# Third layer's modulation moved from the second feed-forward into the second layer's value projection

## The chip, the cores and the metric

The kernel runs on one core of a Trainium2 chip. The metric is the device time of one launch in microseconds. The kernel before took 1823.88 us in the median of three runs (1822.57 to 1826.66).

## What is computed

Three layers act on a sequence of 512 tokens of width 1024, with batch 1. Layers 0 and 1 have a mixer and a feed-forward part; layer 2 is a hybrid of attention and a state-space model. Each layer is modulated: a vector computed from a condition `c` scales, shifts and gates the activations.

```python
# layers 0 and 1
mod = silu(c) @ ada_w[i] + ada_b[i]                 # 1024 -> 6 * 1024
sh1, sc1, g1, sh2, sc2, g2 = split(mod, 6)
x = x + g1 * mixer(rms_norm(x) * (1 + sc1) + sh1)   # i = 0: banded attention; i = 1: spatial gating
x = x + g2 * (square(relu(h @ w1)) @ w2)            # h = rms_norm(x) * (1 + sc2) + sh2
# mixer of layer 1
z = gelu(h @ w_in); u, v = split(z, 2)              # 1024 -> 3072 and 3072
y = (u * (W_s rms_norm(v) + b_s)) @ w_out
# layer 2
mod = silu(c_2) @ w_ada + b_ada                     # 1024 -> 3 * 1024
shift, scale, gate = split(mod, 3)
x = x + gate * (concat(attention(h), state_space(h)) @ w_out)
```

The modulation of layer 2 depends on `c_2` alone and is needed only when the norm of layer 2 begins. The tables of the state-space model (powers of exp(lambda dt), and their products with b and c) depend on weights alone and are needed in layer 2.

## The kernel before

All of x lies transposed in on-chip memory as eight tiles `xT` of 128 features by 512 tokens. Large products are made in three passes: each operand is split into a high and a low part, and `mm3` issues high*high, low*high and high*low (lines 145, 146 and 147). Weights come in chunks of 128 x 1024 by `wchunk`: a DMA on SP's queue into one of four `raw` buffers (L156), a copy by ACT that rounds to the high part `wh` (L157), and a subtraction by DVE that leaves the low part `wl` (L160). `wh` and `wl` have three buffers each, so a chunk is prepared when the one three before it has been used.

A unit of modulation (`ada_cols`) makes 512 of its columns on DVE. A DMA brings weights into `araw`; for each of the eight blocks of 128 rows DVE multiplies by the condition and adds to an accumulator in an `nrm_t` buffer (L196 for the first block, L198 for seven more), and one reduction (L200) leaves partial sums. After every second unit `ada_fold` adds them across partitions by two small matmuls (L208) and adds the bias (L211). How many row blocks one DMA brings (`kchunk`) and how many buffers there are (`abufs`) is set by the stage: 4 and 2 in the feed-forward of layer 0, 1 and 2 in that of layer 1. Layer 2 has six units, so 48 DMAs of 256 KB, 6 of L196, 42 of L198, 6 of L200 and 3 folds.

Such units are background work. `n.work` is a list of functions, and a stage calls `bg()` at certain places, which takes the next function from the list and emits its instructions there. The feed-forward of layer 1 calls it after each group of 256 hidden columns (four times in each of four groups) and after each pair of output blocks. In the kernel before its list holds the units of layer 2's modulation, the folds, and 13 units for the state-space tables: `s5_base`, and for each of four sets `s5_set` parts 0, 1 and 2. `s5_base` is a long chain of small operations on DVE that ends in copies, with some products on POOL. Part 0 is products on POOL (L970, L971, and L972 over a whole tile). Part 1 starts with transposes on TensorE (L977) that read POOL's tile `s5_B`, and later has matmuls L990. Part 2 is a recurrence on POOL and a DMA of the tables to DRAM (L1012). The set's tiles have one buffer each.

The place where a function is called gives its instructions their rank. The framework then fixes one order for each engine from an estimated timeline (`schedule_with_timeline_sim`, L1571); on the chip each engine works through its own order and waits at an instruction whose operands are not there. An instruction of low rank may thus be ordered ahead of later-called work when its buffers and inputs are free early.

In layer 1 `layer1` first makes the values: six blocks `cb` of 512 columns, each of four weight chunks `kk`, four token blocks and two rows (L717); the gelu (L720) and a sum of squares on DVE (L722) follow each block. Then come the units u with the spatial product (L746), whose results go into `g_H` and `g_L`, eight buffers each, and the output product. The value stage has no background work in the kernel before. `then_hybrid` (L641) is what reads layer 2's modulation first.

Of the kernel before, what the change touches and what calls it, by code (L numbers as in the profile page):

```python
# [11 lines left out]
F32 = mybir.dt.float32  # L12
# [7 lines left out]
T = 512  # L20
# [87 lines left out]
class Net:  # L108
    def __init__(self, tc, ctx, d):
        self.tc, self.nc, self.d = tc, tc.nc, d  # L110
        self.ctx = ctx
        self.pp = ctx.enter_context(tc.tile_pool(name="pp", bufs=1))
        self.wp = ctx.enter_context(tc.tile_pool(name="wp", bufs=1))
        self.sp = ctx.enter_context(tc.tile_pool(name="sp", bufs=2))
        self.dr = ctx.enter_context(tc.tile_pool(name="dr", bufs=1, space=bass.MemoryType.DRAM))
        self.s5d = [self.dr.tile([128, self.S5W], F32, name=f"s5d{a}") for a in range(4)]
        self.ps = ctx.enter_context(tc.tile_pool(name="ps", bufs=1, space=bass.MemoryType.PSUM))
        self.work = []
        self.apool = None
        self.mod = {}  # L120


# [58 lines left out]
    def ada_cols(self, w, cond, b, bias, out):  # L181

        nc = self.nc
        wr = w.rearrange("(k p) n -> p k n", p=128)
        acc = self.sp.tile([128, T], F32, name="nrm_t")
        kc = self.kchunk
        cv = self.sp.tile([128, 32], F32, name="a_v")[:, 0:8]
        nc.vector.tensor_copy(cv, cond)
        cond = cv
        for h in range(0, KT, kc):  # L190
            v = self.apool.tile([128, kc, T], F32, name="araw", tag="araw", bufs=self.abufs)
            nc.sync.dma_start(v, wr[:, h:h + kc, b * 128:b * 128 + T])
            for i in range(kc):
                k = h + i
                if k == 0:
                    nc.vector.tensor_scalar(acc, v[:, i, :], cond[:, 0:1], None, op0=ALU.mult)  # L196
                else:
                    nc.vector.scalar_tensor_tensor(acc, v[:, i, :], cond[:, k:k + 1], acc, op0=ALU.mult, op1=ALU.add)  # L198

        nc.vector.tensor_reduce(self.folds[:, b // 8 % 2, b % 8:b % 8 + 4, :], acc.rearrange("p (i q c) -> p i q c", i=4, q=4),  # L200
                                axis=AX.X, op=ALU.add, apply_transpose=True)
        if b % 8 == 4:
            self.folding = lambda: self.ada_fold(b - 4, bias, out)
# [442 lines left out]
    def ffn(self, l, then, hold=None):  # L646
        nc, d, tc = self.nc, self.d, self.tc
        mod = self.mods[l]
        w1 = d["ffn_w1"][l].rearrange("(k p) n -> p k n", p=128)
        w2 = d["ffn_w2"][l].rearrange("(k p) n -> p k n", p=128)  # L650
        with ExitStack() as c:
            self.abufs, self.kchunk = (2, 4) if l == 0 else (2, 1)
            fp = self.apool = c.enter_context(tc.tile_pool(name="fp", bufs=1))
            banks = itertools.cycle(["a", "a", "s", "s", "t", "t"])
            for g in range(4):
                gh, gl = [], []
                for m4 in range(4):
                    c0 = g * 1024 + m4 * 256
                    if c0 == 0:
                        accs = self.up_first([(w1[:, :, 0:512], 0)], banks)  # L660
                    elif c0 == 256:
                        accs = []
                    else:
                        ws = [self.wchunk(w1[:, 4 * hf:4 * hf + 4, c0:c0 + 256], 4, 256) for hf in range(2)]
                        accs = self.up(ws, banks)
                    for acc in accs:
                        s = fp.tile([128, T], F32, name="f_s", bufs=3)
                        H = fp.tile([128, T], F32R, name="f_H", bufs=9)
                        L = fp.tile([128, T], F32R, name="f_L", bufs=9)
                        nc.scalar.activation(s, acc, AF.Relu)  # L670
                        nc.vector.scalar_tensor_tensor(s, acc, 0.0, s, op0=ALU.max, op1=ALU.mult)
                        nc.scalar.copy(H, s)
                        nc.vector.tensor_tensor(L, s, H.bitcast(F32), op=ALU.subtract)
                        gh.append(H)
                        gl.append(L)
                    self.bg()
                self.fold()
                for m2 in range(4 if g < 3 else 2):
                    ws = [self.wchunk(w2[:, g * 8 + 4 * hf:g * 8 + 4 * hf + 4, m2 * 256:m2 * 256 + 256], 4, 256)
                          for hf in range(2)]  # L680
                    self.down(m2, lambda k, mi: [x[:, k % 4, mi * 128:mi * 128 + 128] for x in ws[k // 4]],
                              lambda k: (gh[k], gl[k]), 8, mod[:, 40:48], banks)
                    self.bg()
            self.bg(100)
            hold = hold or (lambda m: [fp.tile([128, 1024], F32R, name="w_last", bufs=6) for _ in range(2)])
            self.down_last(w2[:, 24:32, :], lambda k: (gh[k], gl[k]), 8, mod[:, 40:48], banks, then(), hold)


    def layer1(self):
        nc, d, tc = self.nc, self.d, self.tc  # L690
# [1 line left out]
        w_in = d["b_w_in"][0].rearrange("(k p) n -> p k n", p=128)  # L692
        w_out = d["b_w_out"][0].rearrange("(k p) n -> p k n", p=128)
        with ExitStack() as c:
            gp = c.enter_context(tc.tile_pool(name="gp", bufs=1))
            v = [gp.tile([128, 3072], F32, name=f"v{i}") for i in range(4)]
            wsT = gp.tile([128, 8, 128], F32, name="wsT")
            bsb = gp.tile([128, 8, 128], F32, name="bsb")
# [6 lines left out]
            for cb in range(6):  # L705
# [5 lines left out]
                for kk in range(4) if cb else ():  # L711
                    w = self.wchunk(w_in[:, 2 * kk:2 * kk + 2, c0:c0 + 512], 2, 512)
                    for i in range(4):
                        for k2 in range(2):
                            k = 2 * kk + k2
                            self.mm3(accs[i], self.h(k, i * 128, i * 128 + 128), [x[:, k2, :] for x in w],
                                     k == 0, k == KT - 1)  # L717
                for i in range(4):
                    vv = v[i][:, cb * 512:cb * 512 + 512]
                    nc.scalar.activation(vv, accs[i], AF.Gelu)  # L720
# [811 lines left out]
def body(tc, out, **d):  # L1532
    with ExitStack() as ctx:
        n = Net(tc, ctx, d)
# [3 lines left out]
        ada += [lambda b=b: n.ada_layer(1, b) for b in range(12)]  # L1538
        n.work = [f for a in ada for f in (a, n.fold)]
        n.ffn(0, n.then_layer1)  # L1540
        n.layer1()
        with tc.tile_pool(name="s5p", bufs=1) as sp5:
            ada = [f for b in range(6) for f in (lambda b=b: n.ada_layer(2, b), n.fold)]
            s5 = [lambda: n.s5_base(sp5)] + [lambda a=a, q=q: n.s5_set(sp5, a, q) for a in range(4) for q in range(3)]

            n.work = s5[:1] + ada[:3] + s5[1:2] + ada[3:5]
            n.work += [f for p in zip(s5[2:9], ada[5:]) for f in p] + s5[9:]
            held = []

            def hold(m):  # L1550
# [24 lines left out]
```

## Time and profile before

| | |
|---|---|
| median of three runs | 1823.88 us |
| the profiled execution | 1823.5 us, span 1821.3 us |
| TensorE (PE) busy | 1769.0 us, 97% |
| DVE busy | 1126.9 us, 62% |
| ACT, POOL busy | 652.4 us, 453.8 us |
| mean granted TensorE clock | 0.993 of full |

The stages on the span's clock, in us: layer 0 to about 310, its feed-forward to 680, layer 1's values 680 to 820, units and output 820 to 1105, its feed-forward 1105 to 1490, layer 2 from there. A matmul's busy time overlaps the next one's, so the distance from start to start tells the rate: where nothing is missing a 128x512 matmul starts every 0.234 us.

In a windows row the columns are: the stretch, its length, then busy us and instruction count (x) of PE, of PE's weight loads (PEld), DVE, ACT and POOL, then the granted clock, the DMA engines' share and GB/s. In a timeline row: start, duration, engine, line, operation, output and inputs, count, and in brackets the idle time before it and who ended it.

### The profile page before, as it was taken

The numbers are of one execution on the slowest core, as the hardware profiler recorded it, in microseconds if no ns is written. First come the engines' busy times: TensorE is split into PE (matmuls) and PEld (weight loads), VectorE is DVE, ScalarE is ACT, GpSimd is POOL, SyncE is SP. The second block draws the span as 40 slices with busy tenths as digits, with TensorE's granted clock in tenths as the row PEclk, the third lists the DMA queues.
The fourth block names the chain that finished last, engine by engine and source line by source line (L and its number), as shares of the span: only waits on it lengthen the run. The fifth ranks groups of instructions, "written<-read, shape, count | busy, mean of one in ns | idle before, by whom it ended". The sixth has DMA issues, their size and how long they took to land.

```text
span 1821.3 us, 24858 instructions
## 1 busy us (share of the span) xinstructions
PE 1769.0 (97%) x9308; PEld 1418.1 (78%) x9308; DVE 1126.9 (62%) x2153; ACT 652.4 (36%) x1159; POOL 453.8 (25%) x625
## 2 busy tenths in 40 slices
PE   7999999999999999999999999998999999999998
PEld 4787767887788888888888889886888888786556
DVE  4477866887763445345344457996565554698864
ACT  3345545413231334222223244223233434245642
POOL 0055632000000020001011020048877420144340
PEclk9999999999999999999999999999999999999999
DMA  9554514677643333322322333653444344553101
GB/s 340 168 171 121 172 53 128 196 253 255 221 139 93 104 104 93 93 90 64 102 93 73 105 113 119 196 174 127 140 139 139 125 148 140 172 167 106 47 12 47
DMA packets 197975, 243.06 MB, mean 133 GB/s; under 512 B 18912, under 2 KB 151264, under 8 KB 196192
## 3 DMA queue, kind: packets, MB, share of 16 engines
q1 hardware_dynamic: 194464, 229.77, 40.2%
q10 hardware_dynamic: 3392, 11.71, 1.8%
q8 instruction: 73, 1.20, 0.3%
q14 instruction: 46, 0.38, 0.1%
HBM read 228.87 MB, written 12.58 MB: 133 GB/s over the span
## 4 chain that ended last, share of the span: by engine, by line
PE 77%; DVE 9%; DMA 6%; issue 3%; POOL 2%; ACT 2%; SPq 0%; ACTq 0%; DVEq 0%; POOLq 0%
PE ps_a L145 10%; PE ps_a L146 9%; PE ps_a L147 9%; PE ps_s L146 7%; PE ps_s L145 6%; PE ps_s L147 6%; PE ps_t L146 6%; PE ps_t L145 6%; PE ps_t L147 6%; DMA araw<-in_ada_w 3%; DVE nrm_t L198 2%; DVE wl L160 2%; DMA araw<-in_w_ada 1%; PE ps_s L1474 1%; PE ps_s L592 1%
## 5 line engine op out<-in xcount | busy, mean ns | idle before, releaser
L160 DVE TENSOR_TENSOR wl<-raw,wh 128x1024 fp32r<-128x1024 f32 (+3 forms) x269 | 326.7, 1215 | 277.4 <-ACT wh L157 273.3
L157 ACT ACTIVATE wh<-raw 128x1024 fp32r<-128x1024 f32 (+3 forms) x269 | 275.8, 1025 | 516.3 <-PE ps_a L146 135.7
L146 PE MATMUL ps_a<-hL,wh 128*128 128x512 f32 (+1 forms) x440 | 165.3, 378 | 2.7 <-DVE hL L312 2.3
L145 PE MATMUL ps_a<-hH,wh 128*128 128x512 f32 (+1 forms) x440 | 165.6, 387 | 2.4 <-ACT hH L311 0.8
L147 PE MATMUL ps_a<-hH,wl 128*128 128x512 f32 (+1 forms) x440 | 163.4, 376 | 0.0
L198 DVE SCALAR_TENSOR_TENSOR nrm_t<-araw,a_v,nrm_t 128x512 f32<-128x512 f32 x182 | 143.5, 791 | 28.2 <-DMA araw<-in_ada_w 17.5
L145 PE MATMUL ps_a<-wh,hH 128*128 128x256 f32 (+2 forms) x392 | 125.5, 322 | 2.4 <-ACT hH L311 2.1
L254 POOL TENSOR_TENSOR sq<-sq 128x512 f32<-128x512 f32 x15 | 22.5, 1497 | 411.3 <-ACT sq L250 411.3
L753 POOL TENSOR_TENSOR g_t<-g_t,g_u 128x512 f32<-128x512 f32 x24 | 35.2, 1486 | 358.1 <-DVE g_t L749 352.6
L146 PE MATMUL ps_a<-wl,hH 128*128 128x256 f32 (+2 forms) x392 | 122.6, 313 | 0.7 <-DVE wl L160 0.7
L147 PE MATMUL ps_a<-wh,hL 128*128 128x256 f32 (+2 forms) x392 | 120.0, 311 | 0.0
L146 PE MATMUL ps_s<-hL,wh 128*128 128x512 f32 (+1 forms) x288 | 101.3, 358 | 0.0
L147 PE MATMUL ps_s<-hH,wl 128*128 128x512 f32 (+1 forms) x288 | 101.3, 358 | 0.0
L145 PE MATMUL ps_s<-hH,wh 128*128 128x512 f32 (+1 forms) x288 | 97.3, 359 | 0.0
L145 PEld LDWEIGHTS ps_a<-hH,wh 128*128 128x128 f32 x440 | 81.0, 188 | 20.7 <-issue 2.5
L145 PE MATMUL ps_t<-hH,wh 128*128 128x512 f32 (+1 forms) x248 | 96.8, 390 | 0.0
L146 PEld LDWEIGHTS ps_a<-hL,wh 128*128 128x128 f32 x440 | 83.1, 189 | 17.5 <-DVE hL L312 2.7
L146 PE MATMUL ps_t<-hL,wh 128*128 128x512 f32 (+1 forms) x248 | 96.7, 390 | 0.0
L147 PE MATMUL ps_t<-hH,wl 128*128 128x512 f32 (+1 forms) x248 | 96.0, 389 | 0.0
L147 PEld LDWEIGHTS ps_a<-hH,wl 128*128 128x128 f32 x440 | 82.9, 188 | 15.9
L145 PEld LDWEIGHTS ps_a<-wh,hH 128*128 128x128 f32 x392 | 74.0, 189 | 18.4 <-issue 9.8
L320 DVE SCALAR_TENSOR_TENSOR xT<-ps_a,mod,xT 128x512 f32<-128x512 f32 (+1 forms) x65 | 44.7, 691 | 60.2 <-PE ps_a L147 60.1
(576 smaller groups left out, 4296.9 us busy)
## 6 DMA issues: line engine op xcount, KB each, us to landing
raw<-in_ffn_w SPq DMA_DIRECT2D x128, 512.0 KB, 3.8
araw<-in_ada_w SPq DMA_DIRECT2D x28, 1024.0 KB, 5.8
raw<-in_b_w_in SPq DMA_DIRECT2D x48, 512.0 KB, 3.7
araw<-in_ada_w SPq DMA_DIRECT2D x64, 256.0 KB, 3.3
raw<-in_a_w_in SPq DMA_DIRECT2D x28, 512.0 KB, 4.0
raw<-in_b_w_out SPq DMA_DIRECT2D x32, 384.0 KB, 3.0
araw<-in_w_ada SPq DMA_DIRECT2D x48, 256.0 KB, 3.2
s5d<-s_tab ACTq DMA_DIRECT2D x4, 2048.0 KB, 8.3
```

The source lines that it names most:

```text
L145: mm(out, ah, bh, start=start, stop=False)
L146: mm(out, ah, bl, start=False, stop=False)
L147: mm(out, al, bh, start=False, stop=stop)
L157: nc.scalar.activation(wh[:, :k * n], raw[:, :k * n], AF.Copy)
L160: eng.tensor_tensor(wl[:, :k * n], raw[:, :k * n], wh[:, :k * n].bitcast(F32), op=ALU.subtract)
L198: nc.vector.scalar_tensor_tensor(acc, v[:, i, :], cond[:, k:k + 1], acc, op0=ALU.mult, op1=ALU.add)
L254: add(acc, acc, sq, op=ALU.add)
L320: self.nc.vector.scalar_tensor_tensor(x, acc, gate, x, op0=ALU.mult, op1=ALU.add)
L592: nc.tensor.matmul(ss[e][:, :n], qT[rows, i * 128:i * 128 + 128], kT[rows, :n], start=True, stop=True)
L753: nc.gpsimd.tensor_tensor(t, t, u, op=ALU.mult)
L1474: nc.tensor.matmul(ss[e][:, :n], qrT[rows, p, i * 128:i * 128 + 128], kd[rows, 2 * b + g, :n], start=True, stop=False)
```

## The change

The six units and folds of layer 2's modulation go into the work list ahead of `layer1` and are called in its value stage, two functions for each block `cb`; their `araw` tiles take the eight buffers of `g_H`, with one row block to a DMA. In the feed-forward of layer 1 the list holds the 13 state-space units alone, with an empty function after each. `s5_set` part 1 of the first set is thus called at the fifth place and no longer at the eighth; the last unit stays at the 25th.

```diff
@@ class Net
+        self.atag = "araw"
@@ ada_cols
-            v = self.apool.tile([128, kc, T], F32, name="araw", tag="araw", bufs=self.abufs)
+            v = self.apool.tile([128, kc, T], F32, name="araw", tag=self.atag, bufs=self.abufs)
@@ ffn
-            self.abufs, self.kchunk = (2, 4) if l == 0 else (2, 1)
+            self.abufs, self.kchunk = 2, 4
@@ layer1
-            gp = c.enter_context(tc.tile_pool(name="gp", bufs=1))
+            gp = self.apool = c.enter_context(tc.tile_pool(name="gp", bufs=1))
+
+            self.abufs, self.kchunk, self.atag = 8, 1, "g_H"
...
                             self.mm3(accs[i], self.h(k, i * 128, i * 128 + 128), [x[:, k2, :] for x in w],
                                      k == 0, k == KT - 1)
+                    self.bg(kk % 2)
+                self.bg(0 if cb else 2)
@@ body
+        n.work = [f for b in range(6) for f in (lambda b=b: n.ada_layer(2, b), n.fold)]
         n.layer1()
         with tc.tile_pool(name="s5p", bufs=1) as sp5:
-            ada = [f for b in range(6) for f in (lambda b=b: n.ada_layer(2, b), n.fold)]
             s5 = [lambda: n.s5_base(sp5)] + [lambda a=a, q=q: n.s5_set(sp5, a, q) for a in range(4) for q in range(3)]
-            n.work = s5[:1] + ada[:3] + s5[1:2] + ada[3:5]
-            n.work += [f for p in zip(s5[2:9], ada[5:]) for f in p] + s5[9:]
+            none = lambda: None
+            n.work = [f for u in s5 for f in (u, none)]
```

## Rows read from the trace of the kernel before

**Rows 1.** The page: busy shares, and the granted TensorE clock in 40 slices.

```profile
PE 1769.0 (97%) x9308; PEld 1418.1 (78%) x9308; DVE 1126.9 (62%) x2153; ACT 652.4 (36%) x1159; POOL 453.8 (25%) x625
PEclk9999999999999999999999999999999999999999
```

**Rows 2.** Busy time by stretch: values, feed-forward of layer 1, and of layer 0.

```profile
700.00:820.00 120.00, 120.00 (x515) 96.53 (x515) 46.86 (x86) 37.01 (x45) 0.00 (x0) 1.00 0.32 96
1125.00:1227.00 102.00, 102.00 (x461) 83.06 (x460) 95.67 (x248) 31.90 (x43) 17.23 (x24) 1.00 0.62 190
1227.00:1257.00 30.00, 23.42 (x95) 18.10 (x94) 25.52 (x29) 8.87 (x13) 29.92 (x39) 0.92 0.50 158
...
1300.00:1450.00 150.00, 150.00 (x682) 121.97 (x681) 84.74 (x95) 54.92 (x77) 107.68 (x190) 1.00 0.37 121
310.00:480.00 170.00, 166.75 (x803) 137.29 (x802) 143.12 (x231) 52.75 (x74) 0.00 (x0) 1.00 0.72 235
...
1244.67:1258.93 14.26, 7.68 (x23) 5.42 (x22) 10.33 (x11) 1.86 (x4) 13.95 (x23) 0.76 0.31 104
```

**Rows 3.** Waits of PE from 1090 to 1520 (total us, times, longest).

```profile
PE ps_c L977 <- POOL s_B L972: 4.5, 1, 4.5
...
PE ps_a L147 <- DVE wl L160: 2.1, 1, 2.1
```

**Rows 4.** Timeline of PE around both of these waits, and the second set's transposes.

```profile
1244.67 0.40 PE L146 MATMUL ps_a<-f_L,wh 128*128 128x512 f32 x1
1247.16 0.50 PE L147 MATMUL ps_a<-f_H,wl 128*128 128x512 f32 x1 [2.09 <-DVE wl L160]
...
1250.91 0.63 PE L146 MATMUL ps_a<-f_L,wh 128*128 128x512 f32 x1
1256.04 1.11 PE L977 MATMUL ps_c<-ident,s_B 128*128 128x128 f32 x4 [4.49 <-POOL s_B L972]
...
1258.93 0.39 PE L145 MATMUL ps_a<-f_H,wh 128*128 128x512 f32 x1
...
1262.90 0.60 PE L977 MATMUL ps_c<-ident,s_B 128*128 128x128 f32 x4
...
1309.48 0.60 PE L977 MATMUL ps_c<-ident,s_B 128*128 128x128 f32 x4
```

**Rows 5.** Timeline of DVE just ahead of the first wait.

```profile
1242.80 3.15 DVE L673 TENSOR_TENSOR f_L<-f_s,f_H 128x512 fp32r<-128x512 f32 x1
1245.87 1.23 DVE L160 TENSOR_TENSOR wl<-raw,wh 128x1024 fp32r<-128x1024 f32 x1
```

**Rows 6.** Timeline of POOL: its start, and ends of part 0 of two sets.

```profile
1204.15 2.73 POOL L847 TENSOR_TENSOR s_ct<-s_scr,s_bc 128x512 f32<-128x512 f32 x1 [100.56 <-DVE s_scr L901]
...
1242.26 3.14 POOL L972 TENSOR_TENSOR s_c<-s_c,s_ct 128x1152 f32<-128x1152 f32 x1
...
1252.80 3.18 POOL L972 TENSOR_TENSOR s_B<-s_B,s_ct 128x1024 f32<-128x1024 f32 x1
...
1302.97 2.25 POOL L972 TENSOR_TENSOR s_B<-s_B,s_ct 128x1024 f32<-128x1024 f32 x1
```

**Rows 7.** Groups of DVE instructions from 1105 to 1257: the modulation's.

```profile
L198 DVE SCALAR_TENSOR_TENSOR nrm_t<-araw,a_v,nrm_t 128x512 f32<-128x512 f32 x42 | 33.0, 786 | 9.4 <-DMA araw<-in_w_ada 9.3
...
L200 DVE TRANSPOSE_TENSOR_REDUCE folds<-nrm_t 128x16 f32<-128x512 f32 x6 | 4.2, 702 | 0.0
...
L196 DVE TENSOR_SCALAR nrm_t<-araw,a_v 128x512 f32<-128x512 f32 x6 | 3.9, 646 | 0.0
```

**Rows 8.** All instructions on the tile araw from 1100 to 1260: SP's issues.

```profile
L192 SPq DMA_DIRECT2D araw<-in_w_ada x48: 327/328/445, 1103.9 to 1247.8; - x48
```

**Rows 9.** Timeline of DVE in the value stage: one of its weight subtractions.

```profile
717.93 1.23 DVE L160 TENSOR_TENSOR wl<-raw,wh 128x1024 fp32r<-128x1024 f32 x1 [4.37 <-ACT wh L157]
```

**Rows 10.** Waits of PE in layer 0's feed-forward, 310 to 480.

```profile
PE ps_a L145 <- ACT f_H L672: 1.6, 1, 1.6
PE ps_a L147 <- DVE wl L160: 0.9, 1, 0.9
```

## The prediction

> **What bounds the kernel now.** I read the page first. TensorE is busy for 1769.0 us of the span of 1821.3 us and its clock is at full speed in all but a few stretches [rows 1], so only a stretch in which TensorE stands can give time back; DVE's 62% is an average over stages and says nothing by itself. The second view is busy time by stretch. In layer 1's value stage (700 to 820) PE is busy throughout and DVE for only 46.9 of 120 us. In the first 100 us of layer 1's feed-forward (1125 to 1227) DVE is at 95.7 of 102 us, yet PE loses nothing. From 1227 to 1257 PE has 23.4 of 30 us, and the granted clock is 0.92 [rows 2]. The third view, PE's waits, names two there: 2.1 us for a `wl` of DVE and 4.5 us for the `s_B` of POOL that the first set's transposes read [rows 3]. The fourth is the timeline of PE around them, and it gives the price. After the matmul of 1244.67 the next starts at 1247.16. The one at 1250.91 takes 0.63 us where 0.39 is usual. The transposes come only at 1256.04, and the usual pace is back at 1258.93 [rows 4]. The stretch between 1244.67 and 1258.93 has a granted clock of 0.76 on average [rows 2], which is a mixture of the two levels, 1.2 and 2.4 GHz; ahead of the fall PE had stood for the wait of 2.1 us.
>
> The usual pace can be read just behind: 17 starts of 512-column matmuls lie between 1258.93 and 1262.90, 0.234 us each [rows 4]. In the 14.26 us of the bad stretch I count 19 such matmuls (18 records and one that is missing from the pattern), 4.45 us, and four transposes, which take 0.36 us at full clock. So 14.26 - 4.81 = **9.4 us** are lost there: 4.5 + 2.1 us of standing and 2.8 us of slow clock and restart. Nothing else in this feed-forward is worth a term.
>
> **What the change does to this stretch.** Two chains meet in it, and DVE is the head of both. POOL began its work on the tables only at 1204.15, after 100.6 us of waiting for the last step of `s5_base` on DVE [rows 6]. All of that time DVE also carried layer 2's modulation: 42 products of 786 ns, six first products and six reductions, 33.0 + 3.9 + 4.2 = 41.1 us between 1105 and 1257, and 9.3 us of standing for the `araw` landings [rows 7]. Its transfers, 48 issues of 0.33 us on SP, end at 1247.8 [rows 8], although in the list the last unit has the 19th place, which at some 11 us a place is called about 70 us later: low rank does not hold them back.
>
> Taken out, they shorten the chain. Of the 152 us in which they lie, 99 are before 1204; taken in proportion that is 27 us of work and 6 of standing, so `s5_base` ends about 30 us earlier, and POOL's part 0 with it, at about 1225 and not 1256. TensorE's order is made anew for this, so being earlier is worth nothing in itself: what counts is how late POOL is against the place that the order gives the transposes. In the first set it was late by 4.5 us, and PE itself had been held up before by 2.5 us and by seven slow matmuls of 0.2 us each, so by some 8 us. In the second set, with no modulation on DVE, PE came to the transposes at 1309.48 and POOL had ended at 1302.97 + 2.25 = 1305.22 [rows 4, 6], 4.3 us ahead. The difference between a set with the modulation and one without is about 12 us, of which the waits for landings explain about half and the crowding on DVE the rest. I take it that the first set becomes like the second, but `s5_base` still shares DVE with the subtractions and collides with POOL, so I keep **1.0 us** as a remainder of this wait. Its bounds are 0 (as in the second set) and 9.4 - 2.5 = 6.9 us, all of the bad stretch but the wait for `wl`.
>
> The wait for `wl` came from one operation: `f_L` took 3.15 us from 1242.80, and the subtraction behind it in DVE's order started at 1245.87 [rows 5]. The products of the same size on `araw` take 0.79 us [rows 7]. POOL ran its product over the whole tile from 1242.26 to 1245.40 [rows 6]. The Trainium skill, page "SBUF — State Buffer", section "Who interferes with whom", says that DVE operations with two inputs in SBUF and GpSimd operations share one pair of ports under an exclusive lock, so that the second to start is blocked until the first is done. The trace agrees: `f_L` ended about 0.6 us after POOL did. That rule speaks against the change, since all eight such products of POOL remain; it is the second rival below. For the sum I go by the stretch 1300 to 1450, with six of them and PE busy for 150.0 of 150 us [rows 2]: DVE, at 84.7 of 150 there, prepares weights far enough ahead to absorb 3 us.
>
> **What it costs in the value stage.** There the units bring 41.1 us on DVE [rows 7], with a little for three folds, 48 issues on SP (16 us, [rows 8]) and three pairs of small matmuls on PE, which cost the same in either place. DVE has 120 - 46.9 = 73 us free [rows 2], so it holds them. They will be packed at the front, about 75 us of a DVE near 95% busy, since eight buffers let transfers run a unit ahead. Behind a product that waits for its landing stand `wl` subtractions, and PE waits for those. The cover is their lead: DVE waits 4.37 us for ACT before a subtraction, which ACT starts when PE frees a buffer [rows 9]. With three buffers and 24 matmuls of 0.234 us to a chunk, a subtraction has two chunks, 11.2 us, less 2.3 us for ACT and itself: 9 us. All of DVE's waits for landings in the feed-forward sum to 9.3 us [rows 7], 1.6 us a unit. On SP, four `raw` buffers lie 22 us ahead, against 2 MB of `araw`, 8.9 us at the 235 GB/s of layer 0's feed-forward [rows 2]. POOL does nothing there, so it can block nobody. If the cover fails, the nearest case is layer 0's feed-forward: 14 units in 1 MB transfers, DVE at 143 of 170 us, and PE lost 0.9 us for a `wl` and 1.6 us for an `f_H`, of a kind that the value stage lacks [rows 2, 10]. For six units of the 14 that is 0 to 1.1 us; I take **0.5 us**. A gain here is excluded: PE has no idle time to give.
>
> **The rest costs nothing.** The empty functions emit no instruction. `kchunk` of 4 in layer 1's feed-forward has no unit left to apply to. The `g_H` buffers are read by DVE long before the first `g_H` is written at about 830. POOL's sets follow one another by their buffers, not by the list, so they end earlier; the weights held for the last block find their buffers free earlier, and PE did not wait for those anyway. Layer 2 keeps its order of work, as far as a new estimate of all queues leaves it so: 0, with 1 us to either side.
>
> **Sum.** On the profiled execution, 1823.5 - 9.4 + 1.0 + 0.5 = 1815.6 us. The median of the runs is 0.4 us above that execution, so **1816.0 us**, 0.43% faster. Its own range goes from 1823.9 - 9.4 - 1 = 1813.5, less a microsecond for the spread of the runs, to 1819.
>
> **Rivals.** (1) The transposes find POOL late again, since a dense chain of small dependent operations on DVE may run slower than estimated. For it: the first set's order rests on an estimate that was 8 us too early. Against it: three later sets with no such wait. It costs the upper bound, 6.9 instead of 1.0 us: 1821.9 us. (2) A product of POOL blocks DVE again just ahead of a `wl` that is due, now without the modulation. For it: rows 5. Against it: six products later without harm. It costs 2.5 us and the slow matmuls behind it, 1.4: 1819.9 us. (3) The other side: in the value stage, L198 waits for `araw` behind a burst of transfers and holds a `wl` past its 9 us, so that PE stands. One such hold as in rows 4 costs 2.5 + 1.4 = 3.9 us. If each of six units does this, 23 us come on and the time is 1839 us; with three of them the gain is gone. It decides from the point where waits and products in one run exceed 9 us: a unit's 6.9 us of products and 1.6 us of waiting come close. Against it: at 95.7 of 102 us of DVE, with the same 48 transfers and two buffers only, PE lost nothing from 1125 to 1227 [rows 2]. (4) The change doesn't do what it says: the units are ordered so late that they run into the scaling of the values by L731 and its followers at 817, or the chain of `s5_base` is as long without them. Then PE gives back what it gains: about 1823.9 us.
>
> **How the numbers follow.** The forecast has 0.66, rival 1 0.13, rival 2 0.07, rival 3 0.09, rival 4 0.05. A measurement of this kernel can tell about 0.2%, 3.6 us, from no change, so faster means under 1820.2: the forecast and most of rival 2, 0.72. Rivals 1 and 4 and the rest of 2 are the same, 0.18; rival 3 and a tail are slower, 0.10. The range reaches from 1812.5 over rivals 2 and 1 to 1822.5 and leaves out rivals 3 and 4 and some of the tails.
>
> **What would show it.** Right: in the profile after, no product on `araw` behind 830; DVE near 95% from 700 to 775 and PE with no wait there; POOL's first product of `s5_base` at about 1165 on the old clock; no wait of L977 over 1 us, and no fall of the clock between 1110 and 1480. Wrong: PE waiting for `wl` in the value stage (rival 3), for `s_B` (rival 1), or a block of DVE by POOL that PE follows (rival 2).

## The result, and the profile after

The changed kernel takes 1811.8 us in the median (1810.47 to 1815.38), the kernel before 1824.7 in the same comparison: a ratio of 0.9938, with an interval of 0.9921 to 0.9954 (this ratio is the recorded one; the quotient of the two medians is 0.9929). The profiled execution is one of 1812.79 us, with a span of 1810.7; against the profiled execution of before that is 10.7 us less. Forecast were 1816.0 us and 7.9 us less, and a range from 1812.5 to 1822.5: the median is 0.7 us below its low end. In the code after, the lines up to layer 1 stand one lower (`wl` is L161, the modulation L197, L199 and L201), those behind it five (the transposes are L982, POOL's products over a tile L977).

The page of the changed kernel: busy time, and the granted TensorE clock. PE has 4.5 us less of busy time than before [rows 1], though it computes the same. A standing PE isn't busy, so this is not the waits: in the bad stretch PE was busy for 7.68 us [rows 2] with what takes 4.81 at the usual pace, so slow matmuls there had taken 2.9 of the 4.5 us.

```profile
PE 1764.5 (97%) x9308; PEld 1414.4 (78%) x9308; DVE 1123.7 (62%) x2153; ACT 651.6 (36%) x1159; POOL 447.2 (25%) x625
PEclk9999999999999999999999999999999999999999
```

Busy time by stretch, with the columns of [rows 2]: the front of the value stage, and the two stretches of the feed-forward.

```profile
700.00:725.00 25.00, 25.00 (x110) 20.17 (x109) 22.68 (x40) 9.56 (x12) 0.00 (x0) 1.00 0.94 317
725.00:750.00 25.00, 25.00 (x108) 20.09 (x107) 23.24 (x44) 6.54 (x8) 0.00 (x0) 1.00 0.83 287
750.00:775.00 25.00, 25.00 (x110) 20.17 (x109) 14.07 (x25) 7.59 (x9) 0.00 (x0) 1.00 0.34 106
1125.00:1227.00 102.00, 102.00 (x466) 83.05 (x465) 76.49 (x202) 34.15 (x47) 49.95 (x82) 1.00 0.32 98
1227.00:1257.00 30.00, 30.00 (x139) 24.43 (x138) 21.15 (x23) 12.68 (x18) 23.95 (x34) 1.00 0.44 142
```

DVE is now 91% and 93% busy in the first 50 of these 75 us, the DMA engines 94% and 83%, and PE loses nothing. The last product is done at 756, some 58 us after the first at 698; I had expected about 75 us. The bad stretch of 1227 to 1257, where PE had 23.42 us at a clock of 0.92 [rows 2], has 30.00 at 1.00.

The modulation's products in the value stage, as groups of DVE (busy us, mean ns | idle before them and who ended it). They take 0.75 us each, where those in the feed-forward took 0.79 in the mean [rows 7], and their landings make DVE stand for 4.0 us, at the beginnings of units only.

```profile
L199 DVE SCALAR_TENSOR_TENSOR nrm_t<-araw,a_v,nrm_t 128x512 f32<-128x512 f32 x42 | 30.3, 746 | 0.2
L197 DVE TENSOR_SCALAR nrm_t<-araw,a_v 128x512 f32<-128x512 f32 x6 | 2.9, 484 | 4.0 <-DMA araw<-in_w_ada 4.0
```

PE's waits from 1090 to 1520, where [rows 3] had 4.5 us for `s_B` and 2.1 for `wl`. Neither is there. Of the three that are left, the two at `hL` and `hH` belong to the norm of layer 2, and the one at `sqh` stands at 1105.71, in the norm ahead of this feed-forward.

```profile
PE ps_a L147 <- DVE hL L313: 1.9, 1, 1.9
PE ps_c L269 <- ACT sqh L264: 0.8, 1, 0.8
PE ps_a L146 <- ACT hH L312: 0.7, 1, 0.7
```

Timeline of POOL: its first product, and the end of part 0 of the first set, which answer to [rows 6].

```profile
1171.51 1.52 POOL L852 TENSOR_TENSOR s_ct<-s_scr,s_bc 128x512 f32<-128x512 f32 x1 [67.48 <-DVE s_scr L906]
...
1208.65 2.23 POOL L977 TENSOR_TENSOR s_B<-s_B,s_ct 128x1024 f32<-128x1024 f32 x1
```

Timeline of PE: the transposes that read it start 1.29 us behind its end of 1210.88, with no wait ahead of them.

```profile
1212.17 0.60 PE L982 MATMUL ps_c<-ident,s_B 128*128 128x128 f32 x4
```

Timeline of DVE: the subtraction that ran into that product of POOL takes 2.47 us and not 1.2.

```profile
1209.50 2.47 DVE L161 TENSOR_TENSOR wl<-raw,wh 128x1024 fp32r<-128x1024 f32 x1 [0.25 <-ACT wh L158]
```

To place the gain I cut both traces at PE's starts. The feed-forward of layer 1 is counted from its first 256-column matmul on `hH` to that of layer 2. Timeline of PE before:

```profile
1105.42 0.50 PE L145 MATMUL ps_a<-hH,wh 128*128 128x256 f32 x2
...
1489.03 0.39 PE L145 MATMUL ps_a<-hH,wh 128*128 128x256 f32 x1 [0.66 <-ACT hH L311]
```

Timeline of PE after:

```profile
1106.23 0.50 PE L146 MATMUL ps_a<-hH,wh 128*128 128x256 f32 x2
...
1479.47 0.39 PE L146 MATMUL ps_a<-hH,wh 128*128 128x256 f32 x1 [0.66 <-ACT hH L312]
```

That is 383.6 us before and 373.2 after: 10.4 us less, of 10.6 in the span. Cut in the same way, from the last matmul of layer 0's feed-forward, the value and units stages together take 430.6 us before and 431.6 after; the rest is below 1.3 us in any stage.

### The profile page after: what moved, and what is told of

It reads as the page before. It is cut to its first block, busy times and chain, and to the rows that moved or that the text cites. A ratio compares the mean times of both kernels' runs of the same rounds, so it can differ in the third digit from the quotient of the medians.

```text
span 1810.7 us, 24870 instructions
## 1 busy us (share of the span) xinstructions
PE 1764.5 (97%) x9308; PEld 1414.4 (78%) x9308; DVE 1123.7 (62%) x2153; ACT 651.6 (36%) x1159; POOL 447.2 (25%) x625
## 4 chain that ended last, share of the span: by engine, by line
PE 84%; DVE 6%; DMA 6%; ACT 2%; issue 2%; POOL 1%; ACTq 0%; SPq 0%; DVEq 0%; POOLq 0%
PE ps_a L146 11%; PE ps_a L147 10%; PE ps_a L148 10%; PE ps_s L147 7%; PE ps_s L148 7%; PE ps_s L146 7%; PE ps_t L147 7%; PE ps_t L146 7%; PE ps_t L148 7%; DMA araw<-in_ada_w 4%; DVE nrm_t L199 2%; PE ps_s L1479 1%; PE ps_s L593 1%; DVE wl L161 1%; PE ps_o L620 1%
## 5 line engine op out<-in xcount | busy, mean ns | idle before, releaser
L161 DVE TENSOR_TENSOR wl<-raw,wh 128x1024 fp32r<-128x1024 f32 (+3 forms) x269 | 325.9, 1212 | 264.2 <-ACT wh L158 260.1
L199 DVE SCALAR_TENSOR_TENSOR nrm_t<-araw,a_v,nrm_t 128x512 f32<-128x512 f32 x182 | 140.7, 781 | 19.0 <-DMA araw<-in_ada_w 17.6
## 6 DMA issues: line engine op xcount, KB each, us to landing
raw<-in_b_w_out SPq DMA_DIRECT2D x32, 384.0 KB, 3.0
```

Of the source, the lines that this page charges most:

```text
L161: eng.tensor_tensor(wl[:, :k * n], raw[:, :k * n], wh[:, :k * n].bitcast(F32), op=ALU.subtract)
```

## Experiments

All times are medians, compared with the kernel before on the same chip (1824.5 to 1825.1 us in five comparisons). In the table, "landings" is the time for which DVE stood for the modulation's transfers, in the stage into which the run puts them; "feed-forward" and "values and units" are cut from the profiled execution as above.

| kernel | median us | ratio, interval | landings us | feed-forward us | values and units us |
|---|---|---|---|---|---|
| before | 1824.7 | 1 | 9.3 | 383.6 | 430.6 |
| after | 1811.8 | 0.9938 [0.9921, 0.9954] | 4.0 | 373.2 | 431.6 |
| places of before | 1812.04 | 0.9931 [0.9919, 0.9943] | | 373.2 | 431.6 |
| spacing alone | 1824.06 | 1.0001 [0.9991, 1.0011] | 9.9 | 386.1 | 430.6 |
| no modulation | 1815.09 | 0.9951 [0.9937, 0.9964] | 0 | 373.4 | 431.0 |
| products, no transfers | 1815.13 | 0.9947 [0.9934, 0.996] | 0 | 374.2 | 431.7 |
| transfers, tiny products | 1824.94 | 1.0004 [0.9993, 1.0016] | 23.7 | 384.0 | 431.2 |
| tiny products alone | 1814.31 | 0.9938 [0.9918, 0.9958] | 0 | 374.9 | 431.7 |
| transfers alone | 1814.29 | 0.9942 [0.9925, 0.9959] | 0 | 376.1 | 431.2 |
| before, three buffers | 1815.53 | 0.9956 [0.994, 0.9971] | 2.0 | 378.4 | 430.6 |
| values, doubled | 1815.4 | 0.9953 [0.9935, 0.997] | 7.1 | 374.5 | 431.9 |
| values, three buffers | 1816.54 | 0.9963 [0.9949, 0.9977] | 21.2 | 373.2 | 435.4 |
| values, one buffer | 1832.16 | 1.0049 [1.0029, 1.0069] | 80.6 | 373.1 | 453.8 |
| two more units | 1811.86 | 0.994 [0.9923, 0.9957] | 3.6 | 373.3 | 431.8 |

### The two halves of the change

The move and the new spacing come together. The first run keeps the move and puts the state-space units back to their old places.

```diff
-            n.work = [f for u in s5 for f in (u, none)]
+            n.work = s5[:1] + [none] * 3 + s5[1:2] + [none] * 2
+            n.work += [f for u in s5[2:9] for f in (u, none)] + s5[9:]
```

> The modulation is moved as in the change, but the 13 state-space units stay at their places of before (1, 5, 8, 10, ... 20, 22 to 25), with empty functions where the modulation's were. Theory A, that the relief of DVE alone makes the gain: as the changed kernel, 1811 to 1815 us, PE waits under 1 us for s_B and none for wl in layer 1's feed-forward, first transposes within 3 us of 1212. Rival B, that the earlier call of part 1 (fifth place and not eighth) matters: 1817 to 1824 us, with a wait for s_B or the first transposes 20 us later.

Measured: 1812.04 us, the feed-forward 373.2 us, no wait for `s_B` or `wl`. The second run leaves the modulation in the feed-forward of the kernel before and only spaces the units.

```diff
-            n.work = s5[:1] + ada[:3] + s5[1:2] + ada[3:5]
-            n.work += [f for p in zip(s5[2:9], ada[5:]) for f in p] + s5[9:]
+            n.work = [f for p in zip(s5, ada) for f in p] + s5[12:]
```

> The modulation stays in layer 1's feed-forward with its two buffers, but the state-space units take every second place, as in the change, with the modulation's functions between them. Theory A: DVE is as crowded as before, POOL's chain starts near 1204, the first transposes find POOL late by 3 to 6 us and the clock falls: 1820 to 1826 us. Rival B: the places make the gain, 1811 to 1816 us with no such wait.

Measured: 1824.06 us. PE's waits from 690 to 1520 in it:

```profile
PE ps_c L977 <- POOL s_B L972: 6.3, 1, 6.3
PE ps_a L147 <- DVE wl L160: 2.4, 1, 2.4
```

Both waits are there, longer than before. The move is the whole gain, and the spacing is nothing.

### No modulation at all

The third run takes the six units out (the modulation of layer 2 is left out and set to zero).

```diff
-        n.work = [f for b in range(6) for f in (lambda b=b: n.ada_layer(2, b), n.fold)]
+        n.nc.vector.memset(n.mods[2], 0.0)
```

> As the changed kernel, but layer 2's modulation is left out and set to zero: no products, transfers or folds in the value stage. Theory A, that the value stage hides it wholly: the changed kernel's 1811.8 us less 0.6 us for six small matmuls, 1810 to 1813 us. Rival C, that it still costs something there that no wait of PE shows: 1805 to 1809 us.

Measured: 1815.09 us, some 2 us above my range. Where the modulation had been it shows what was asked: feed-forward 373.4 us, value stage with units 431.0. So the units in the value stage cost 0.7 us. It goes with the pairs of fold matmuls, which left the feed-forward: from the last matmul of layer 0's feed-forward to the first spatial product it takes 148.24 us without a pair, 148.90 with three (148.93 with doubled units) and 149.11 with four (two more units). The 2 us are in layer 2, 3.6 us longer in the profiled execution than after, though only its input differs; at its beginning PE waits 3.1 us for `hH`, at the place where it waits 1.9 us for `hL` after.

### Crowding or landings

In the prediction I had shared the lateness of POOL between DVE's waits for landings and its crowding, half and half. This run adds to the changed kernel, in layer 1's feed-forward and at the old places, six units of the same DVE operations on a resident tile, with no transfer; nobody uses their results.

```diff
+            ada = [f for b in range(6) for f in (lambda b=b: n.dve_unit(b), none)]
+            n.work = s5[:1] + ada[:3] + s5[1:2] + ada[3:5]
+            n.work += [f for p in zip(s5[2:9], ada[5:]) for f in p] + s5[9:]
...
+                nc.vector.scalar_tensor_tensor(acc, self.fsrc, cv[:, k:k + 1], acc, op0=ALU.mult, op1=ALU.add)
```

> As the changed kernel, but in layer 1's feed-forward six units of DVE work of the same shape as the modulation's are added at its old places (1 copy, 8 products of 128x512, 1 reduction each), reading a tile that lies on the chip: the crowding without transfers. If the late landings make POOL late against its order (half of it by my sum): POOL starts near 1200 but the wait for s_B is 0 to 2 us and the time 1812 to 1817 us. Rival D, that crowding and collisions with POOL alone do it: wait 3.5 to 5.5 us and a fall of the clock, 1819 to 1824 us.

Measured: 1815.13 us. Busy time by stretch, and PE's one wait of that kind:

```profile
1125.00:1227.00 102.00, 102.00 (x460) 82.91 (x459) 95.75 (x231) 32.73 (x43) 5.87 (x5) 1.00 0.31 94
1227.00:1257.00 30.00, 30.00 (x130) 24.17 (x129) 25.39 (x44) 10.18 (x14) 24.96 (x40) 1.00 0.28 88
```

```profile
PE ps_c L998 <- POOL s_B L993: 0.3, 1, 0.3
```

Timeline of POOL, its first product:

```profile
1217.38 1.06 POOL L868 TENSOR_TENSOR s_ct<-s_scr,s_bc 128x512 f32<-128x512 f32 x1 [114.72 <-DVE s_scr L922]
```

DVE is as crowded as before (95.75 of 102 us against 95.67, [rows 2]) and POOL starts 13 us later than before [rows 6]; yet PE stands for 0.3 us, and the feed-forward is only 0.9 us longer than after. So neither crowding nor a late POOL costs much by itself. I take it that this is because the order of PE is made for both; the run doesn't show the reason. The other half is the opposite: 48 transfers through two buffers at the old places, each with a product on 128x16 elements only.

```diff
+        for k in range(KT):
+            v = self.apool.tile([128, 1, T], F32, name="araw", bufs=2)
+            nc.sync.dma_start(v, wr[:, k:k + 1, b * 512:b * 512 + T])
+            nc.vector.tensor_scalar(acc[:, 16 * k:16 * k + 16], v[:, 0, 0:16], 2.0, None, op0=ALU.mult)
```

> The changed kernel with, in layer 1's feed-forward, the 48 transfers of layer 2's modulation weights once more, at the places of the kernel before and through two buffers, but with only a 128x16 product on DVE for each, whose result nobody reads. Nothing of the computation is left out. Theory (DVE stands for landings that come later than the fixed order assumed): DVE is nearly free of the 41 us of products, yet PE waits for s_B or wl again for some 3 to 7 us, and the time is 1815 to 1822 us. Rival (it takes crowding of DVE as well as landings): no wait above 1 us, 1811 to 1814 us.

Measured: 1824.94 us, all of the gain gone, with DVE at 77.90 of 102 us. Waits of DVE (1105 to 1260):

```profile
DVE nrm_t L653 <- DMA araw<-in_w_ada: 23.7, 21, 3.5
```

Waits of PE:

```profile
PE ps_t L148 <- DVE wl L161: 6.3, 1, 6.3
...
PE ps_s L148 <- DVE wl L161: 1.7, 1, 1.7
```

Timeline of DVE ahead of PE's longest wait, which ends at 1208.59:

```profile
1194.74 0.30 DVE L653 TENSOR_SCALAR nrm_t<-araw 128x16 f32<-128x16 f32 x1 [0.16 <-DMA araw<-in_w_ada]
1198.56 2.37 DVE L653 TENSOR_SCALAR nrm_t<-araw 128x16 f32<-128x16 f32 x1 [3.52 <-DMA araw<-in_w_ada]
1200.85 0.74 DVE L321 SCALAR_TENSOR_TENSOR xT<-ps_s,mod,xT 128x512 f32<-128x512 f32 x1
1201.51 0.28 DVE L653 TENSOR_SCALAR nrm_t<-araw 128x16 f32<-128x16 f32 x1
1203.65 3.67 DVE L653 TENSOR_SCALAR nrm_t<-araw 128x16 f32<-128x16 f32 x2 [1.86 <-DMA araw<-in_w_ada]
1207.23 1.30 DVE L161 TENSOR_TENSOR wl<-raw,wh 128x1024 fp32r<-128x1024 f32 x1
```

Timeline of POOL in the same run:

```profile
1198.19 2.67 POOL L985 TENSOR_TENSOR s_c<-s_c,s_ct 128x1152 f32<-128x1152 f32 x1
...
1205.04 2.21 POOL L985 TENSOR_TENSOR s_B<-s_B,s_ct 128x1024 f32<-128x1024 f32 x1
```

The `wl` that PE needs stands in DVE's order behind products that stand for their landings (3.52 and 1.86 us). The products, 0.175 us in the median of the 48, take 2.37 us and 3.67 for two where a product of POOL runs. So this run has two suspects besides the landings: the tiny products that POOL blocks, and the transfers' own traffic. Two more runs try them one by one. The one has no transfers, and its products read a resident tile in place of `araw`; the other drops the products.

```diff
...
-            v = self.apool.tile([128, 1, T], F32, name="araw", bufs=2)
-            nc.sync.dma_start(v, wr[:, k:k + 1, b * 512:b * 512 + T])
-            nc.vector.tensor_scalar(acc[:, 16 * k:16 * k + 16], v[:, 0, 0:16], 2.0, None, op0=ALU.mult)
+            nc.vector.tensor_scalar(acc[:, 16 * k:16 * k + 16], self.fsrc[:, 0:16], 2.0, None, op0=ALU.mult)
```

> The run with 48 transfers and tiny products (1824.9 us), with the products kept at their places but reading a resident tile, and no transfers. Nothing of the computation is left out. Theory (waits for landings make the standing): without them PE waits for neither wl nor s_B, and the time is 1811 to 1815 us. Rival (the tiny products themselves, blocked by POOL's products for some 2 us at a time, hold the weight subtractions): PE waits 3 us or more for wl and the time is 1817 to 1825 us.

```diff
             nc.sync.dma_start(v, wr[:, k:k + 1, b * 512:b * 512 + T])
-            nc.vector.tensor_scalar(acc[:, 16 * k:16 * k + 16], v[:, 0, 0:16], 2.0, None, op0=ALU.mult)
```

> The same run with the 48 transfers kept, two buffers, but no product on DVE: nobody reads what lands. Theory (the transfers cost nothing by their own traffic, only by what DVE waits for): 1811 to 1815 us, with no wait of PE for a weight. Rival (the traffic or SP's queue delays the weights themselves): PE waits for wl or wh, behind a weight transfer that lands late, and the time is 1817 to 1825 us.

Measured: 1814.31 and 1814.29 us. PE's waits for weights in the first and in the second:

```profile
PE ps_s L148 <- DVE wl L161: 0.2, 1, 0.2
```

```profile
PE ps_s L146 <- ACT wh L158: 1.0, 1, 1.0
```

The transfers with tiny products add 10.8 us to the feed-forward, the products alone 1.7 and the transfers alone 2.9. Of these two, 1.2 and 1.5 us lie in the first 48 us of the feed-forward, where the granted clock falls right behind the norm. That fall isn't made by the added work: the run with doubled values (below), which adds nothing to this stage, has it too, and with it 1.3 us in the same place. Busy time there after, with the products alone, and with doubled values:

```profile
1105.00:1112.00 7.00, 6.29 (x50) 6.10 (x51) 4.90 (x22) 2.30 (x5) 0.00 (x0) 1.00 0.50 161
1105.00:1112.00 7.00, 6.65 (x42) 6.57 (x43) 4.64 (x22) 2.17 (x5) 0.00 (x0) 0.76 0.48 160
1105.00:1112.00 7.00, 7.00 (x47) 7.00 (x47) 3.90 (x18) 1.13 (x3) 0.00 (x0) 0.76 0.34 134
```

So the products alone cost some 0.4 us, and the transfers alone some 1.4, of which 1.0 is the wait for `wh`. But the first of the two runs doesn't test its rival, products that POOL blocks. With nothing to wait for, the products (ns least/median/most, first and last start) all stand ahead of POOL's first product, which comes at 1176.00, and none is blocked:

```profile
L653 DVE TENSOR_SCALAR nrm_t<-fsrc x48: 166/168/175, 1127.5 to 1139.2; 128x16 f32<-128x16 f32 x48
```

What costs is thus products that wait for their landings. With their transfers they are spread from 1123 to 1227, among POOL's products, and the subtraction comes behind landings and blocks. Between the end of the subtraction before (1193.45) and the one of 1207.23 DVE stood 6.2 us for landings, and the three blocked products took 5.5 us more than usual. How much of PE's 6.3 us is due to the one and to the other no run here parts.

### The old place with one more buffer

If so, the kernel before can be mended where it is. The edit is to its buffers alone.

```diff
-            self.abufs, self.kchunk = (2, 4) if l == 0 else (2, 1)
+            self.abufs, self.kchunk = (2, 4) if l == 0 else (3, 1)
```

> The kernel before with three buffers and not two for the modulation's transfers in layer 1's feed-forward, nothing else. Theory (late landings make the standing): DVE's waits for landings shrink from 9.3 us, PE's wait for s_B shrinks with them, and the time falls by 2 to 9 us, to 1815 to 1822 us. Rival (a transfer is ordered as early as its buffer lets it, so that one more buffer only moves the same waits ahead; or the waits are not the cause): 1823 to 1826 us with s_B still at 3 us or more.

Measured: 1815.53 us. DVE's wait for landings from 1105 to 1260, and PE's for `s_B`:

```profile
DVE nrm_t L198 <- DMA araw<-in_w_ada: 2.0, 3, 0.9
```

```profile
PE ps_c L977 <- POOL s_B L972: 2.4, 1, 2.4
```

Busy time of the stretch around that wait:

```profile
1259.00:1267.00 8.00, 5.59 (x21) 4.32 (x20) 1.41 (x1) 1.54 (x2) 7.61 (x16) 0.79 0.02 6
```

One buffer takes 7.3 of 9.3 us of landings away, and half of the loss in the feed-forward (378.4 us, against 383.6 and 373.2). The crowding stays (97.58 of 102 us), POOL begins at 1215.16, 11 us later than before, and what is left of lateness is still followed by a standing of 2.4 us and a fall of the granted clock to a mean of 0.79 between its two levels. This refutes the rival expectation, with the products and their places in the work list as before. It isn't the landings alone that change, though: the engines' orders are made anew, and 87 of DVE's 340 instructions from 1100 to 1270 stand in another place.

### How far the value stage covers

Rival 3 had put a price on the value stage. Three runs load it: each unit emitted twice, three buffers and not eight, and one.

```diff
-        n.work = [f for b in range(6) for f in (lambda b=b: n.ada_layer(2, b), n.fold)]
+        n.work = [f for b in range(6) for f in (lambda b=b: (n.ada_layer(2, b), n.ada_layer(2, b)), n.fold)]
```

> The changed kernel with each of the six modulation units in the value stage emitted twice (96 transfers, 84 products); the results are the same. DVE has 47 us of its own work and 2 x 41 us of modulation, 130 of the stage's 120 us. Theory (the value stage hides the units only because DVE has 73 us to spare there): the work does not fit, weight subtractions or the scaling of the values come late, and the stage and what follows grow by 10 us or more: 1820 to 1835 us. Rival (the products slide behind the stage into the units stage, where DVE also has room, and PE loses nothing): 1811 to 1815 us.

```diff
-            self.abufs, self.kchunk, self.atag = 8, 1, "g_H"
+            self.abufs, self.kchunk, self.atag = 3, 1, "g_u"
```

> The changed kernel with three buffers (those of g_u) and not eight for the modulation's transfers in the value stage. Theory (a landing hurts only where it is later than the lead of the weight subtractions behind it, about 9 us): DVE stands longer for landings than the 4 us of the changed kernel, but each for 1 to 3 us only; no wait of PE in the value stage, 1811 to 1815 us. Rival (eight buffers are what hides the units there; with three it goes as with two in the feed-forward): PE waits for wl in the value stage and 3 to 10 us are lost, 1815 to 1822 us.

```diff
-            self.abufs, self.kchunk, self.atag = 8, 1, "g_H"
+            self.abufs, self.kchunk, self.atag = 1, 1, "araw"
```

> The changed kernel with a single buffer for the modulation's transfers in the value stage, so that each of 48 transfers is issued only when the product before it is done, and lands 3 us or more later. Theory: DVE stands 48 times for some 2.5 to 4 us, 120 to 190 us, against 73 us that it has free there; several of these in a row exceed the 9 us of lead, PE waits for wl, and the time is 1830 us or more. Rival (the order is made for such a chain, subtractions are put between the products and PE never notices): 1811 to 1816 us.

Doubled: my theory fell. Busy time in two of its stretches:

```profile
750.00:775.00 25.00, 25.00 (x109) 20.11 (x108) 23.77 (x41) 6.53 (x8) 0.00 (x0) 1.00 0.90 308
775.00:800.00 25.00, 25.00 (x110) 20.16 (x109) 23.78 (x46) 7.19 (x9) 0.00 (x0) 1.00 0.96 320
```

With DVE 95% busy from 750 to 800 and the DMA engines at 90 and 96%, PE loses nothing, and values and units take 431.9 us. The last product begins at 807.8, ahead of the scaling of the values, which begins at 816.6. The order puts subtractions between the products: the longest stretch from one subtraction to the next with products in it is 8.7 us, as in the changed kernel. The median of 1815.4 us is above that of the change, but the profiled execution has 1.3 us more in the feed-forward (the fall of the clock behind the norm, above), 3.2 in layer 2 and 0.3 here.

Three buffers: 1816.54 us, as the rival said. DVE's and PE's waits in the value stage:

```profile
DVE nrm_t L199 <- DMA araw<-in_w_ada: 19.5, 15, 3.2
```

```profile
PE ps_t L147 <- DVE wl L161: 2.9, 3, 1.4
```

Timeline of DVE ahead of the first of these three, which ends at 765.73:

```profile
759.28 2.33 DVE L199 SCALAR_TENSOR_TENSOR nrm_t<-araw,a_v,nrm_t 128x512 f32<-128x512 f32 x3 [2.12 <-DMA araw<-in_w_ada]
...
764.05 0.49 DVE L197 TENSOR_SCALAR nrm_t<-araw,a_v 128x512 f32<-128x512 f32 x1 [1.70 <-DMA araw<-in_w_ada]
764.46 1.22 DVE L161 TENSOR_TENSOR wl<-raw,wh 128x1024 fp32r<-128x1024 f32 x1
```

One buffer: 1832.16 us, slower than before, as the theory said. What DVE stood for most, up to the end of the units, and PE's two largest waits:

```profile
DVE nrm_t L199 <- DMA araw<-in_w_ada: 75.4, 39, 3.7
```

```profile
PE ps_c L209 <- DVE a_v L189: 7.7, 2, 3.9
PE ps_s L147 <- DVE wl L161: 2.6, 2, 1.8
```

Values and units lengthen by 3.7 us with 21.2 us of landings and by 22.2 with 80.6. With one buffer PE stands most at the fold's matmul, whose partial sums DVE makes too late (3.75 us at 756.89, 3.94 at 816.39), and at both of these the clock falls: the granted clock is 0.66 from 756 to 761 and 0.57 from 814 to 822.

### Two more units

The last run moves two of layer 1's own units, needed only in its feed-forward, out of layer 0's feed-forward, where PE lost 3.25 of 170 us with 14 of them [rows 2]. Four more functions are called behind the first block of the value stage.

```diff
-                self.bg(0 if cb else 2)
+                self.bg(0 if cb else 6)
...
-        ada += [lambda b=b: n.ada_layer(1, b) for b in range(12)]
+        ada += [lambda b=b: n.ada_layer(1, b) for b in range(10)]
...
-        n.work = [f for b in range(6) for f in (lambda b=b: n.ada_layer(2, b), n.fold)]
+        n.work = [f for l, b in [(2, b) for b in range(6)] + [(1, 10), (1, 11)]
+                  for f in (lambda l=l, b=b: n.ada_layer(l, b), n.fold)]
```

> The changed kernel with two of layer 1's own modulation units (the last two, needed only in its feed-forward) moved from layer 0's feed-forward into the value stage behind the six of layer 2: 12 units stay in layer 0's feed-forward, where PE lost some 3.5 us with 14 of them, and DVE has 47 + 55 = 102 of 120 us in the value stage. Theory (a stage gains only where its landings come late against its order): layer 0's feed-forward gives back 0 to 3.5 us and the value stage stays hidden: 1808 to 1812 us. Rival (at 102 of 120 us the value stage is no longer hidden): 1813 to 1820 us.

Measured: 1811.86 us, no change against after. The value stage hides eight units (431.8 us); layer 0's feed-forward is 0.8 us shorter in the profiled execution, but between kernels that share its code it went from 364.5 to 369.0 us, so this doesn't tell. No kernel tried is better than the change.

## Why the prediction was right, and where it was off

**The bad stretch (-9.4 us): right.** Both waits and the slow clock are gone, the feed-forward shortens by 10.4 us, and 0.7 of this are the fold matmuls that went with the units, if they cost there what they cost in the value stage. POOL's first product comes 32.6 us earlier, at 1171.5; I had said 30, and "about 1165" where the marks are listed, which doesn't agree with the 30 and was 6 us off.

**The remainder of 1.0 us at the first transposes: not there.** The slack is 1.3 us and no wait. I had kept it because `s5_base` shares DVE with the subtractions and collides with POOL; the collisions are there (rival 2 below), and no wait of PE follows them. The split ahead of it, landings for half of the lateness and crowding for the other half, failed as well: crowding alone adds 0.9 us to the feed-forward and tiny products with landings 10.8. A product's duration is in the estimate from which each engine's order is fixed; the orders of DVE, POOL and PE are made for it together. A transfer that lands later than its place in DVE's order is not, and it shifts DVE and, through `wl` or through POOL's `s_B`, PE. That the estimate has the landings too early is inferred. The runs show that where DVE stood for landings in the feed-forward, this stage was 5 to 13 us longer than after, and where it did not, at most 2.9. The loss doesn't follow the length of the standing, since every run has an order of its own: 9.9 us of landings (spacing alone) go with 12.9 us more than after, 23.7 with 10.8. In the kernel before itself, DVE stood for a landing some 5 us ahead of the blocked `f_L` of [rows 5], with a subtraction right behind:

```profile
1237.92 0.79 DVE L198 SCALAR_TENSOR_TENSOR nrm_t<-araw,a_v,nrm_t 128x512 f32<-128x512 f32 x1 [2.26 <-DMA araw<-in_w_ada]
```

That such landings made POOL's `s_B` late there is argued from the other runs and not shown by itself.

**The value stage (+0.5 us): no wait there, but not for my reason.** Values and units are 1.0 us longer than before and 0.7 longer than without modulation, by the fold matmuls; the prediction had these as equal in either place, and what they add here the feed-forward lost. I had argued that a subtraction has a lead of 9 us over the PE that needs it, so that landings of 1.6 us can't reach PE. With three buffers no single standing of DVE is over 3.2 us, and PE still waits three times for a `wl`. The lead is what the buffers permit; DVE's order uses it for products, several in a row, and landings add up before the next subtraction: 2.12 and 1.70 us ahead of the first of the three waits, 0.55 and 2.58 ahead of the second. The third has none between, only what was late already. What covers the stage is that the landings are early: eight buffers let them run ahead to 4.0 us of standing in all. My remark on two buffers in the feed-forward, at which PE lost nothing from 1125 to 1227, was no evidence for that: the loss came in one piece behind that stretch.

**Rival 3** (a `wl` held in the value stage) has the right mechanism, and one buffer shows it; its point of decision, products and waits over 9 us in one run, is wrong. With three buffers PE waits behind runs of 7.3, 6.1 and 5.9 us from one subtraction to the next, and after the change a run of 8.7 us costs nothing. Doubled products don't reach 9 us, so they test only whether the units fit. **Rival 2** (POOL blocks DVE ahead of a due `wl`) happens three times, at 1209.50, 1253.11 and 1304.61, with 2.47, 2.48 and 2.51 us for the subtraction, and PE notices none of them. As the prediction said, DVE is ahead there. **Rivals 1 and 4** did not occur.

**The size.** The forecast was 4.2 us above the median. From profiled execution to profiled execution it had 7.9 us of gain, where 10.7 are measured: 1.5 of the difference are the two remainders, 1.2 are layer 2, which took 327.6 us before and 326.3 after. The other 1.4 us are medians against single executions: 0.4 at the kernel before, 1.0 at the one after (1812.79 against 1811.8). Layer 2 is the open part. In single profiled executions of these kernels, with its code unchanged, it took 325.3 to 332.2 us, counted to PE's last transposes. The granted clock goes with it: from the start of layer 2 to the end its mean is 0.99 in the execution of 325.3 us (tiny products alone), in that of before and in that of the change, and 0.97 in the one of 332.2 us (products, no transfers). Four runs whose feed-forward, values and units are within 1.7 us of the change's have medians of 1814.3 to 1815.4 us, and three others, the change among them, 1811.8 to 1812.0. Whether the last 2 or 3 us are the change's own or a lucky course of layer 2 no run here settles.

## What to carry to other kernels

Where each engine works through a fixed order, ask of background work not how busy it makes its engine but what it waits for: 41 us of resident products cost 0.9 us, and 48 tiny ones (8 us where nothing blocks them) that wait for transfers 10.8. Such work goes where there are buffers enough for its transfers to land ahead of its place, and one buffer more may bring half of what a move brings. A lead that buffers permit is no lead that the order keeps, so sum the landings between two due operations and don't take them one by one.

## What was not expected of the hardware

A one-input product on 128x16 elements, 0.175 us in the median, took 2.37 us while POOL ran a product over a whole tile, and ended with it. The Trainium skill, page "SBUF — State Buffer", section "Who interferes with whom", lists `tensor_scalar` among the operations that may use the ports shared with GpSimd, so that the block depends on who is first and not on size; the trace agrees (1198.56 to 1200.93 on DVE, 1198.19 to 1200.86 on POOL). In the profile such a block is no wait: it stands in the duration of the blocked operation, and counts as busy.

48 transfers of 256 KB, with 189 GB/s in all between 1125 and 1227, that nobody waits for cost the feed-forward of 373 us some 1.4 us, 1.0 of them as a wait for a weight.

Behind the same norm the clock fell in some executions and not in others: PE's wait for `sqh` ahead of it was 0.82 us in the changed kernel, where the granted clock stayed at 1.00 from 1105 to 1112, and 0.82 us with the tiny products alone, where it was 0.76. Such a fall costs 1.2 to 1.5 us of the length of a stage, so a difference of that size between single profiled executions may be nothing else.
